# First layer's experts of a two-layer backbone: the row of g2 for each slot comes from a two-row table in DRAM, by a gather per block

## The chip, the cores and the metric

The kernel runs on one core of a Trainium2 chip. The metric is the device time of one execution in microseconds (us); the median of a few runs stands for a kernel.

## The reference, cut to what matters

The backbone has two layers. Each layer mixes tokens and then sends every token through two of 16 experts (a hierarchical mixture of experts). A vector g2 of 1024 numbers scales what the experts add. In the first layer there are two such vectors: one for the 256 context tokens and one for the 1024 latent tokens. In the second layer only latent tokens are left, and so one vector.

```
def expert_block(args):
    xblk, e = args
    return (jax.nn.silu(xblk @ w1[e]) * (xblk @ w3[e])) @ w2[e]
...
out = jnp.zeros((n_tok + 1, d), h.dtype).at[slot_tok].add(yb * slot_w[:, None])
...
if last:
    x = x + g2 * hier_moe(h2, *moe_args).reshape(bsz, n_lat, d)
else:
    f = hier_moe(jnp.concatenate([h2c, h2], axis=0), *moe_args)
    ctx = ctx + cg2 * f[:bsz * n_ctx].reshape(bsz, n_ctx, d)
    x = x + g2 * f[bsz * n_ctx:].reshape(bsz, n_lat, d)
```

The kernel does it slot by slot: each row of an expert's result `y` is multiplied by its slot's weight and by the g2 row of the slot's token, and is added into `xb`, the tokens in DRAM.

## The kernel before

**The expert stage.** It runs from about 940 to 1530 us for the first layer and from about 2320 to 2880 us for the second. The order of the code is the order of the instructions on each engine (a manual schedule). The experts come in the order `eo`, called e0 to e15 here. Every expert has a main block of 128 slots (`block` with `x0`). Ahead of it an expert with many tokens has a full block for its next 128 slots (`x1`) and one more block (`x2`), which is half (64 rows, `block_half`) where few slots are left; an expert with a few tokens too many has one half block; and the others have the main block alone. I call an expert with the main block alone a light one: e0, e2, e4, e6, e8, e12, e14 and e15. In all the first layer runs 29 blocks: 22 of 128 rows and 7 of 64.

**What a main block does.** TensorE forms `hps` from the slots' activations `x` and the weights `ew`, then `yps` (y, in PSUM) from `ghl` and more of `ew`. Each product is made of three matmuls, for which both factors are split into a high and a low part. Around it, `side(u)` prepares the next expert. SyncE fetches its 12 weight units (`eraw`, 512 KB each, 8 buffers). ScalarE copies the high part (L1579). VectorE subtracts for the low part (L1581), for every third unit GpSimd. The rows of later experts are gathered from DRAM on GpSimd's queue (`xg`, L1591 and L1869), and are transposed on TensorE (`xtp`) and split into `x` (L63, L64 and L1611).

**How a block ends.** `gain` makes the row of factors `yt`, and `scatter` multiplies it with y and adds the product into `xb` by an indirect DMA on GpSimd's queue (L1627). The tile `yt` has three buffers, which are given out in the order of the code; as that falls, all main blocks have the same one of the three, and the `x1`, `x2` and half blocks use the others. In the first layer `gain` combines both vectors, which stand broadcast in SBUF: `sw` holds the weight of the slots of latent tokens (0 for the others), `swc` that of context tokens:

```
nc.scalar.activation(out=yt[0:n], in_=g2b[1][0:n], func=AF.Copy, scale=wc[0:n])
nc.vector.scalar_tensor_tensor(out=yt[0:n], in0=g2b[0][0:n], scalar=w[0:n], in1=yt[0:n], op0=OP.mult, op1=OP.add)
...
nc.vector.tensor_tensor(out=yt[0:n], in0=y[0:n], in1=yt[0:n], op=OP.mult)
```

In the second layer there is one vector, and a single operation multiplies y, weight and vector (L1624).

**After the last block** of the first layer comes the second layer's front: SyncE and ScalarE load the tokens back from `xb` (`xf`, L283), ScalarE squares them (L290), SyncE loads weights of the modulation (L241) for TensorE (`modps`, L244), and TensorE transposes the tokens (`tp`, L305).

Of the kernel before, what the change touches and what calls it, by code (L numbers as in the profile page):

```python
# [9 lines left out]
F32 = mybir.dt.float32  # L10
# [10 lines left out]
P = 128  # L21
# [34 lines left out]
def backbone_kernel(ctx: ExitStack, tc: tile.TileContext, x, ctx_in, cond, w_mod, b_mod, norm1, norm2, w_in_t, w_in_vg,  # L56
# [91 lines left out]
    for l in range(depth):  # L148
# [1404 lines left out]
        with ExitStack() as st:  # L1553
# [8 lines left out]
            for c in ((0,) if last else (0, 1)):  # L1562
                g2b[c] = mp1.tile([P, D], F32, name=f"g2{c}")
            swc = sw if last else mp1.tile([P, NB * NE], F32, name="swc")
# [50 lines left out]
            def gain(n, w, wc):  # L1615
                yt = wk.tile([P, D], F32, name="yt", tag="yt", bufs=YT)
                if not last:
                    nc.scalar.activation(out=yt[0:n], in_=g2b[1][0:n], func=AF.Copy, scale=wc[0:n])
                    nc.vector.scalar_tensor_tensor(out=yt[0:n], in0=g2b[0][0:n], scalar=w[0:n], in1=yt[0:n], op0=OP.mult, op1=OP.add)
                return yt  # L1620

            def scatter(yt, y, n, w, yidx):
                if last:
                    nc.vector.scalar_tensor_tensor(out=yt[0:n], in0=y[0:n], scalar=w[0:n], in1=g2b[0][0:n], op0=OP.mult, op1=OP.mult)  # L1624
                else:
                    nc.vector.tensor_tensor(out=yt[0:n], in0=y[0:n], in1=yt[0:n], op=OP.mult)  # L1626
                nc.gpsimd.indirect_dma_start(out=xb, out_offset=bass.IndirectOffsetOnAxis(ap=yidx[0:n], axis=0),  # L1627
                                             in_=yt[0:n], in_offset=None, compute_op=OP.add)

            def block(xt, units, wl_, wc_, yidx, side, s, end=None):  # L1630
# [12 lines left out]
                gs = []  # L1643
                for hf in range(2):
# [16 lines left out]
                for f in range(4):  # L1661
                    w = units[8 + f]
                    for n in range(2):
# [5 lines left out]
                        if (f, n) == (2, 0):  # L1669
                            yt = gain(P, wl_, wc_)  # L1670
# [7 lines left out]
            def block_half(xt, units, wl_, wc_, yidx):  # L1678
# [3 lines left out]
                s = wk.tile([P, D], F32, name="s", tag="yt", bufs=YT)  # L1682
                gs = []
# [37 lines left out]
                yt = gain(R, wl_, wc_)  # L1721
# [98 lines left out]
            for ei, e in enumerate(eo):  # L1820
                x0, x1, x2 = xt_[ei % 2], xt_[2], xt_[(ei + 1) % 2]
                with tc.If(cnt > P + P // 2) as big:
# [8 lines left out]
                    block(x1, units, sw[:, col(e, 1)], swc[:, col(e, 1)], yx[:, col(e, 1)], side1, "e")  # L1831
                    with tc.If(cnt > 2 * P + P // 2) as big2:
                        block(x2, units, sw[:, col(e, 2)], swc[:, col(e, 2)], yx[:, col(e, 2)], idle, "e")
                        with tc.If(cnt > 3 * P):
# [5 lines left out]
                            with tc.For_i(e * cap + 3 * P, e * cap + cnt, P) as i:  # L1840
# [7 lines left out]
                                if not last:  # L1848
                                    nc.vector.tensor_scalar(out=sd[:, 0:1], in0=sd[:, 0:1], scalar1=float(NCTX), scalar2=None, op0=OP.is_lt)
                                    nc.vector.tensor_tensor(out=sd[:, 1:2], in0=sd[:, 0:1], in1=sd[:, 2:3], op=OP.mult)  # L1850
                                    nc.vector.tensor_tensor(out=sd[:, 2:3], in0=sd[:, 2:3], in1=sd[:, 1:2], op=OP.subtract)
                                block(x1, units, sd[:, 2:3], sd[:, 1:2], si[:, 1:2], idle, "e")
                    with big2.Else():
                        with tc.If(cnt > 2 * P):
                            block_half(x2, units, sw[:, col(e, 2)], swc[:, col(e, 2)], yx[:, col(e, 2)])
                with big.Else():
                    with tc.If(cnt > P):  # L1857
                        block_half(x1, units, sw[:, col(e, 1)], swc[:, col(e, 1)], yx[:, col(e, 1)])
# [25 lines left out]
                block(x0, units, sw[:, col(e, 0)], swc[:, col(e, 0)], yx[:, col(e, 0)], side, "")  # L1884
# [139 lines left out]
```

## Time and profile before

| | before |
|---|---|
| median of 3 runs (lowest, highest) | 2894.35 us (2894.32, 2902.83) |
| the profiled execution, its span | 2908.22 us, 2906.5 us |
| busy: TensorE, VectorE, ScalarE, GpSimd | 87%, 63%, 43%, 31% of the span |
| mean granted TensorE clock | 0.934 |

The profile is one execution. Its span is what the rows below are times in, counted from the span's start; 1.7 us of its time lie outside the span. In the rows, an engine's line with a bracket at its end shows how long the engine sat idle before the instruction, and behind `<-` what ended that.

### The profile page before, as it was taken

The page shows a single profiled execution, that of the slowest core. Times are in us where ns is not written, and L with a number is a line of the kernel's source. Part 1 is how long each engine was busy: PE and PEld are TensorE (multiplying, and loading weights), DVE is VectorE, ACT ScalarE, POOL GpSimd, SP SyncE. Part 2 cuts the span into 40 slices and gives each one's busy share as a digit, 9 for nine tenths or more (in the row PEclk, how much of TensorE's full clock was granted, in tenths as well). Part 3 has the DMA queues.
Part 4 walks back from the last instruction along what each step waited for, and adds up shares of the span by engine and source line. Part 5 has one row for each costly group of instructions (what it writes and reads, how often), then busy time and mean ns, then how long its engine had stood idle before and what let it go on. Part 6 is the DMA issues. An engine that isn't in the chain of part 4 may idle for free. (4 is left out here: it accounts for less than half of the span.)

```text
span 2906.5 us, 41486 instructions
## 1 busy us (share of the span) xinstructions
PE 2539.1 (87%) x15412; PEld 2132.5 (73%) x15412; DVE 1816.5 (63%) x3175; ACT 1241.8 (43%) x2060; POOL 898.9 (31%) x576
## 2 busy tenths in 40 slices
PE   6999998898896899889887999979989788878875
PEld 3878887787785677667766898868978666656664
DVE  3304765777478667766775227748857866656765
ACT  3322213566234555544554232137743354545443
POOL 0000113302245444544540001122014445545452
PEclk8999999999897999989998999989989899989987
DMA  8373128331225666776774342173122568686765
GB/s 291 126 246 123 70 86 200 64 71 44 103 109 213 226 223 220 256 252 202 244 243 161 125 141 88 70 181 84 37 89 102 224 222 285 202 279 232 249 234 182
DMA packets 159573, 494.06 MB, mean 170 GB/s; under 512 B 18896, under 2 KB 40016, under 8 KB 158768
## 3 DMA queue, kind: packets, MB, share of 16 engines
q1 hardware_dynamic: 110336, 361.14, 37.5%
q0 software_dynamic: 29312, 99.39, 11.8%
q10 hardware_dynamic: 19552, 28.84, 2.7%
q8 instruction: 200, 3.28, 0.5%
q14 instruction: 173, 1.42, 0.2%
HBM read 408.75 MB, written 79.15 MB: 168 GB/s over the span
## 5 line engine op out<-in xcount | busy, mean ns | idle before, releaser
L1581 DVE TENSOR_TENSOR ew<-eraw,ew 128x1024 fp32r<-128x1024 f32 x256 | 433.7, 1713 | 65.2 <-ACT ew L1579 60.1
L1579 ACT ACTIVATE ew<-eraw 128x1024 fp32r<-128x1024 f32 x384 | 390.5, 1054 | 132.4 <-PE hps L69 115.0
L67 PE MATMUL hps<-ew,x 128*128 128x512 f32 x656 | 281.9, 430 | 105.2 <-PEq L1857 100.6
L1581 POOL TENSOR_TENSOR ew<-eraw,ew 128x1024 fp32r<-128x1024 f32 x128 | 334.4, 2622 | 61.1 <-ACT ew L1579 36.1
L212 PE MATMUL ps<-hh,w 128*128 128x256 f32 x2096 | 289.3, 292 | 17.9 <-ACT hh L319 4.7
L212 PEld LDWEIGHTS ps<-hh,w 128*128 128x128 f32 x2096 | 269.0, 197 | 27.7 <-issue 7.9
L69 PE MATMUL hps<-ew,x 128*128 128x512 f32 x656 | 271.2, 413 | 8.3 <-DVE x L64 7.6
L68 PE MATMUL hps<-ew,x 128*128 128x512 f32 x656 | 271.8, 414 | 0.0
L962 DVE TENSOR_REDUCE mx<-S 128x1 f32<-128x1280 f32 (+1 forms) x144 | 196.8, 1370 | 108.2 <-PE S L957 106.8
L1627 POOL DMA_INDIRECT xb<-yt,yx x54 | 131.2, 2430 | 368.6 <-DVE yt L1626 206.0
L67 PEld LDWEIGHTS hps<-ew,x 128*128 128x128 f32 x656 | 132.6, 202 | 139.7 <-issue 105.7
L970 ACT ACTIVATE pe<-S,mx 128x1280 f32<-128x1280 f32 (+1 forms) x144 | 177.4, 1232 | 49.2 <-DVE mx L962 41.2
L956 PE MATMUL S<-kk,qh 128*128 128x512 f32 (+1 forms) x400 | 159.0, 398 | 16.7 <-DMA qh<-qs 8.3
L69 PEld LDWEIGHTS hps<-ew,x 128*128 128x128 f32 x656 | 132.2, 202 | 41.7 <-DVE x L64 10.2
L68 PEld LDWEIGHTS hps<-ew,x 128*128 128x128 f32 x656 | 133.2, 203 | 28.2 <-issue 1.1
L212 PE MATMUL ps<-hl,w 128*128 128x256 f32 x1048 | 149.1, 286 | 0.0
L67 PE MATMUL ps<-wv,hh 128*128 128x256 f32 (+1 forms) x480 | 142.3, 296 | 0.0
L957 PE MATMUL S<-kk,ql 128*128 128x512 f32 (+1 forms) x400 | 141.4, 368 | 0.3 <-DMA ql<-qs 0.3
L69 PE MATMUL yps<-ew,ghl 128*128 128x512 f32 x328 | 132.5, 404 | 8.0 <-DVE ghl L64 8.0
L67 PE MATMUL yps<-ew,ghl 128*128 128x512 f32 x328 | 138.4, 422 | 0.0
L69 PE MATMUL ps<-wv,hl 128*128 128x256 f32 (+1 forms) x480 | 138.1, 288 | 0.0
L68 PE MATMUL ps<-wv,hh 128*128 128x256 f32 (+1 forms) x480 | 137.9, 287 | 0.0
(597 smaller groups left out, 5765.1 us busy)
## 6 DMA issues: line engine op xcount, KB each, us to landing
eraw<-in_experts_dram SPq DMA_DIRECT2D x384, 512.0 KB
s<-in_w_mod_dram SPq DMA_DIRECT2D x91, 512.0 KB
raw<-in_w_in_t_dram SPq DMA_DIRECT2D x28, 512.0 KB
xb<-xt POOLq DMA_DIRECT2D x18, 512.0 KB, 2.9
h2s<-tm POOLq DMA_DIRECT2D x18, 512.0 KB, 2.9
kk<-ks SPq DMA_DIRECT2D x14, 640.0 KB
ks<-shl ACTq DMA_DIRECT2D x16, 512.0 KB
qs<-shl ACTq DMA_DIRECT2D x16, 512.0 KB
```

Of the source, the lines that this page charges most:

```text
L67: nc.tensor.matmul(o, lhsT=lh, rhs=rh, start=start, stop=False)
L68: nc.tensor.matmul(o, lhsT=lh, rhs=rl, start=False, stop=False)
L69: nc.tensor.matmul(o, lhsT=ll, rhs=rh, start=False, stop=stop)
L212: nc.tensor.matmul(ps[:, o:o + 256], lhsT=wt[:, w_, k, :], rhs=h_[ci][:, k, :], start=w_ == 0 and h_ is hh and k == 0, stop=h_ is hl and k ...
L956: nc.tensor.matmul(S[:, j, :n], lhsT=qh[:, m, q1], rhs=kk[:, m, k0:k0 + n], start=True, stop=False)
L957: nc.tensor.matmul(S[:, j, :n], lhsT=ql[:, m, q1], rhs=kk[:, m, k0:k0 + n], start=False, stop=True)
L962: nc.vector.tensor_reduce(out=u["mx", m], in_=u["S", m], axis=AX.X, op=OP.max, negate=True)
L970: nc.scalar.activation(out=pe[:, :nk], in_=u["S", m], func=AF.Exp, bias=u["mx", m], scale=1.0, accum_out=acc)
L1579: nc.scalar.activation(out=w[:, 0, :], in_=raw, func=AF.Copy)
L1581: eng.tensor_tensor(out=w[:, 1, :], in0=raw, in1=w[:, 0, :].bitcast(F32), op=OP.subtract)
L1627: nc.gpsimd.indirect_dma_start(out=xb, out_offset=bass.IndirectOffsetOnAxis(ap=yidx[0:n], axis=0), in_=yt[0:n], in_offset=None, compute_op ...
```

## The change

It touches the first layer's expert stage alone (`not last`). The two broadcast tiles `g2b` and their two loads of 512 KB are gone, and `swc` with two of its three small operations. A table `rows2` in DRAM holds the two vectors (one DMA of 8 KB), and `kx` holds for each slot the number of its row in it, 1 for a context token. `gain` no longer computes: it gathers for each slot its row of the table into `yt`, by an indirect DMA on GpSimd's queue, and it is called at the start of a block where it was called in the block's last third. `scatter` then multiplies y, the weight and that row in one VectorE operation, as the second layer does with its single vector.

```
+                kx = mp1.tile([P, NB * NE], I32, name="kx")
+                rows2 = dram.tile([2, D], F32, name=f"rows2{l}")
+                nc.scalar.dma_start(out=rows2, in_=modd[l, :, 5 * D:6 * D])
...
-            def gain(n, w, wc):
+            def gain(n, wc):
                 yt = wk.tile([P, D], F32, name="yt", tag="yt", bufs=YT)
                 if not last:
-                    nc.scalar.activation(out=yt[0:n], in_=g2b[1][0:n], func=AF.Copy, scale=wc[0:n])
-                    nc.vector.scalar_tensor_tensor(out=yt[0:n], in0=g2b[0][0:n], scalar=w[0:n], in1=yt[0:n], op0=OP.mult, op1=OP.add)
+                    nc.gpsimd.indirect_dma_start(out=yt[0:n], out_offset=None, in_=rows2,
+                                                 in_offset=bass.IndirectOffsetOnAxis(ap=wc[0:n], axis=0))
                 return yt
...
             def scatter(yt, y, n, w, yidx):
-                if last:
-                    nc.vector.scalar_tensor_tensor(out=yt[0:n], in0=y[0:n], scalar=w[0:n], in1=g2b[0][0:n], op0=OP.mult, op1=OP.mult)
-                else:
-                    nc.vector.tensor_tensor(out=yt[0:n], in0=y[0:n], in1=yt[0:n], op=OP.mult)
+                nc.vector.scalar_tensor_tensor(out=yt[0:n], in0=y[0:n], scalar=w[0:n], in1=(g2b[0] if last else yt)[0:n],
+                                               op0=OP.mult, op1=OP.mult)
...
                 gs = []
+                yt = gain(P, wc_)
                 for hf in range(2):
...
-                        if (f, n) == (2, 0):
-                            yt = gain(P, wl_, wc_)
...
                 s = wk.tile([P, D], F32, name="s", tag="yt", bufs=YT)
+                yt = gain(R, wc_)
                 gs = []
...
-                yt = gain(R, wl_, wc_)
...
             if not last:
-                nc.vector.tensor_scalar(out=swc, in0=ix, scalar1=NCTX, scalar2=None, op0=OP.is_lt)
-                nc.vector.tensor_tensor(out=swc, in0=swc, in1=sw, op=OP.mult)
-                nc.vector.tensor_tensor(out=sw, in0=sw, in1=swc, op=OP.subtract)
+                nc.vector.tensor_scalar(out=kx, in0=ix, scalar1=NCTX, scalar2=None, op0=OP.is_lt)
```

Where it moves instructions is seen on two engines. TensorE's order is the same in both kernels.

On GpSimd a main block of the kernel before looks like this, from the read of the expert's count to the split after the scatter (`xg_11524` is the gather for `x2`; the last DMA is the scatter):

```order
L1872 TENSOR_LOAD cnt_i
L1869 DMA xg_11524<-h2s,ix 128x1024
L1581 TENSOR_TENSOR ew<-eraw,ew 128x1024 x2
L1591 DMA xg<-h2s,ix 128x1024
L1581 TENSOR_TENSOR ew<-eraw,ew 128x1024
L1591 DMA xg<-h2s,ix 128x1024
L1627 DMA xb<-yt,yx 1408x1024
L1581 TENSOR_TENSOR ew<-eraw,ew 128x1024
```

The same place in the changed kernel, whose lines are numbered a few lower or higher (`rows_11526` is the table):

```order
L1621 DMA yt<-rows_11526,kx 128x1024
L1869 TENSOR_LOAD cnt_i
L1866 DMA xg_11524<-h2s,ix 128x1024
L1584 TENSOR_TENSOR ew<-eraw,ew 128x1024 x2
L1594 DMA xg<-h2s,ix 128x1024
L1584 TENSOR_TENSOR ew<-eraw,ew 128x1024
L1594 DMA xg<-h2s,ix 128x1024
L1628 DMA xb<-yt,yx 1408x1024
L1584 TENSOR_TENSOR ew<-eraw,ew 128x1024
```

The new gather stands first, ahead of the gather for `x2` and of all four splits of the block.

On VectorE, the end of e0's main block before, from the split behind `ghl` to the final multiply:

```order
L64 TENSOR_TENSOR ghl<-gtp,ghl 128x256
L1581 TENSOR_TENSOR ew<-eraw,ew 128x1024
L64 TENSOR_TENSOR x_11590<-xtp,x_11589 128x512
L1611 TENSOR_TENSOR x_11589<-xtp,x_11589 128x4x64
L1619 SCALAR_TENSOR_TENSOR yt<-g_11525,sw,yt 128x1024
L1581 TENSOR_TENSOR ew<-eraw,ew 128x1024
L64 TENSOR_TENSOR x_11590<-xtp,x_11589 128x512
L1611 TENSOR_TENSOR x_11589<-xtp,x_11589 128x4x64
L1626 TENSOR_TENSOR yt<-yps,yt 128x1024
```

and in the changed kernel:

```order
L64 TENSOR_TENSOR ghl<-gtp,ghl 128x256
L1584 TENSOR_TENSOR ew<-eraw,ew 128x1024
L64 TENSOR_TENSOR x_11590<-xtp,x_11589 128x512
L1614 TENSOR_TENSOR x_11589<-xtp,x_11589 128x4x64
L1584 TENSOR_TENSOR ew<-eraw,ew 128x1024
L64 TENSOR_TENSOR x_11590<-xtp,x_11589 128x512
L1614 TENSOR_TENSOR x_11589<-xtp,x_11589 128x4x64
L1626 SCALAR_TENSOR_TENSOR yt<-yps,sw,yt 128x1024
```

The operation of L1619 has left the queue, and the split of `ew` moves up into its place. The final operation now reads a tile that a DMA fills.

## Rows read from the trace of the kernel before

**Rows 1.** The page: busy time and share of the span, each engine.

```profile
PE 2539.1 (87%) x15412; PEld 2132.5 (73%) x15412; DVE 1816.5 (63%) x3175; ACT 1241.8 (43%) x2060; POOL 898.9 (31%) x576
```

**Rows 2.** Stretches: length, busy PE PEld DVE ACT POOL, clock, DMA share, GB/s.

```profile
960.00:1526.00 566.00, 501.42 (x2336) 395.74 (x2334) 389.29 (x470) 290.92 (x429) 281.67 (x130) 0.94 0.72 232
...
965.70:971.00 5.30, 5.29 (x13) 4.19 (x14) 2.89 (x4) 2.23 (x3) 4.84 (x4) 0.52 0.99 394
```

**Rows 3.** What TensorE waited for, 955 to 1530 us: total, times, longest.

```profile
PE hps L67 <- PEq L1857: 40.3, 7, 10.4
...
PE hps L69 <- DVE x L64: 6.0, 2, 4.5
PE modps L244 <- DVE yt L1626: 4.3, 1, 4.3
PE yps L69 <- DVE ghl L64: 4.1, 4, 2.2
```

**Rows 4.** Instructions of the lines touched, and the second layer's operation: ns min/median/max.

```profile
L1618 ACT ACTIVATE yt<-g,swc x29: 1137/1147/1166, 957.4 to 1523.5; 128x1024 f32<-128x1024 f32 x22, 64x1024 f32<-64x1024 f32 x7
L1619 DVE SCALAR_TENSOR_TENSOR yt<-g,sw,yt x29: 1266/1285/5399, 958.5 to 1524.7; 128x1024 f32<-128x1024 f32 x22, 64x1024 f32<-64x1024 f32 x7
L1626 DVE TENSOR_TENSOR yt<-yps,yt x22: 1208/1211/1225, 965.9 to 1526.1; 128x1024 f32<-128x1024 f32 x22
L1624 DVE SCALAR_TENSOR_TENSOR yt<-yps,sw,g x18: 1270/1272/1283, 2336.1 to 2855.1; 128x1024 f32<-128x1024 f32 x18
```

**Rows 5.** Gathers: ns; landing us, first of L1869, then of `xg` in 950:1530.

```profile
L1591 POOL DMA_INDIRECT xg<-h2s,ix x64: 942/1757/1950, 919.3 to 2821.9; - x64
...
L1869 POOL DMA_INDIRECT xg<-h2s,ix x30: 937/1058/2007, 957.1 to 2837.5; - x30
...
DMA to landing us min/median/max: 3.8/5.1/6.7
...
DMA to landing us min/median/max: 3.8/8.5/10.4
```

**Rows 6.** Timelines of e0's main block: GpSimd, VectorE, TensorE.

```profile
958.11 4.72 POOL L1581 TENSOR_TENSOR ew<-eraw,ew 128x1024 fp32r<-128x1024 f32 x2
...
958.52 5.40 DVE L1619 SCALAR_TENSOR_TENSOR yt<-g,sw,yt 128x1024 f32<-128x1024 f32 x1
963.85 1.21 DVE L1581 TENSOR_TENSOR ew<-eraw,ew 128x1024 fp32r<-128x1024 f32 x1
964.98 0.68 DVE L64 TENSOR_TENSOR x<-xtp,x 128x512 fp32r<-128x512 f32 x1
...
965.71 0.79 PE L69 MATMUL hps<-ew,x 128*128 128x512 f32 x1 [4.47 <-DVE x L64]
```

**Rows 7.** Timelines of e4's main block, a light one: GpSimd, VectorE, TensorE.

```profile
1109.07 0.97 POOL L1869 DMA_INDIRECT xg<-h2s,ix  x1 [8.13 <-DMA eraw<-in_experts_dram]
1110.06 4.75 POOL L1581 TENSOR_TENSOR ew<-eraw,ew 128x1024 fp32r<-128x1024 f32 x2
...
1125.84 2.34 POOL L1627 DMA_INDIRECT xb<-yt,yx  x1 [4.77 <-DVE yt L1626]
...
1111.15 4.76 DVE L1581 TENSOR_TENSOR ew<-eraw,ew 128x1024 fp32r<-128x1024 f32 x1 [0.53 <-ACT ew L1579]
...
1116.30 0.50 PE L69 MATMUL yps<-ew,ghl 128*128 128x512 f32 x1 [2.19 <-DVE ghl L64]
```

**Rows 8.** Timelines of the layer's end: GpSimd, ScalarE, VectorE, TensorE.

```profile
1510.18 2.33 POOL L1627 DMA_INDIRECT xb<-yt,yx  x1 [6.69 <-DVE yt L1626]
...
1527.56 2.31 POOL L1627 DMA_INDIRECT xb<-yt,yx  x1 [12.63 <-DVE yt L1626]
...
1523.48 1.15 ACT L1618 ACTIVATE yt<-g,swc 128x1024 f32<-128x1024 f32 x1 [4.12 <-DMA xb<-yt,yx]
...
1538.27 1.06 ACT L290 ACTIVATE sq<-xf 128x1024 bf16<-128x1024 f32 x1 [11.75 <-DMA xf<-xb]
...
1526.05 1.23 DVE L1626 TENSOR_TENSOR yt<-yps,yt 128x1024 f32<-128x1024 f32 x1
...
1545.36 1.92 PE L244 MATMUL modps<-xf,condT 128*32 128x512 f32 x4 [11.96 <-DMA xf<-in_w_mod_dram]
```

More of the change, by code (lines that the diff above doesn't have):

```diff
@@ L1561, in backbone_kernel @@
             g2b = {}
[L1562 to L1564 removed]
+            if last:
+                g2b[0] = mp1.tile([P, D], F32, name="g20")
+            else:
+                kx = mp1.tile([P, NB * NE], I32, name="kx")
+                rows2 = dram.tile([2, D], F32, name=f"rows2{l}")
+                nc.scalar.dma_start(out=rows2, in_=modd[l, :, 5 * D:6 * D])
             eo = [EPG * g + i for i in range(EPG) for g in (0, 2, 1, 3)]
@@ L1830, in side1 @@
                             p2(u - 10, ("xtp", "hpse")[u - 10])
-                    block(x1, units, sw[:, col(e, 1)], swc[:, col(e, 1)], yx[:, col(e, 1)], side1, "e")
+                    block(x1, units, sw[:, col(e, 1)], None if last else kx[:, col(e, 1)], yx[:, col(e, 1)], side1, "e")
                     with tc.If(cnt > 2 * P + P // 2) as big2:
-                        block(x2, units, sw[:, col(e, 2)], swc[:, col(e, 2)], yx[:, col(e, 2)], idle, "e")
+                        block(x2, units, sw[:, col(e, 2)], None if last else kx[:, col(e, 2)], yx[:, col(e, 2)], idle, "e")
                         with tc.If(cnt > 3 * P):
@@ L1848, in backbone_kernel @@
                                 if not last:
[L1849 to L1852, printed above, removed]
+                                    kd = wk.tile([P, 1], I32, name="kd", tag="kd", bufs=1)
+                                    nc.vector.tensor_scalar(out=kd, in0=sd[:, 0:1], scalar1=float(NCTX), scalar2=None, op0=OP.is_lt)
+                                block(x1, units, sd[:, 2:3], None if last else kd, si[:, 1:2], idle, "e")
                     with big2.Else():
                         with tc.If(cnt > 2 * P):
-                            block_half(x2, units, sw[:, col(e, 2)], swc[:, col(e, 2)], yx[:, col(e, 2)])
+                            block_half(x2, units, sw[:, col(e, 2)], None if last else kx[:, col(e, 2)], yx[:, col(e, 2)])
                 with big.Else():
                     with tc.If(cnt > P):
-                        block_half(x1, units, sw[:, col(e, 1)], swc[:, col(e, 1)], yx[:, col(e, 1)])
+                        block_half(x1, units, sw[:, col(e, 1)], None if last else kx[:, col(e, 1)], yx[:, col(e, 1)])
                 nxt = []
@@ L1883, in backbone_kernel @@
                     break
-                block(x0, units, sw[:, col(e, 0)], swc[:, col(e, 0)], yx[:, col(e, 0)], side, "")
+                block(x0, units, sw[:, col(e, 0)], None if last else kx[:, col(e, 0)], yx[:, col(e, 0)], side, "")
                 if ei + 1 < NE:
```

## The prediction

> **What bounds the kernel now.** I read the engines' shares first. TensorE is busy for 87% of the span, and no other engine for more than 63% [rows 1]. Then the stage that is changed: of the 566 us from 960 to 1526, TensorE is busy for 501.4, VectorE for 389.3, ScalarE for 290.9, GpSimd for 281.7, and the DMA engines for 0.72 of the time [rows 2]. So TensorE sets the time here too, and an operation taken from another engine gives back at most what TensorE waits for that engine. The waits say how much that is. The largest, 40.3 us in 7 times, is for TensorE's own sequencer after branches, which the change leaves alone. For VectorE's splits of `x` and `ghl` it waited 6.0 + 4.1 = 10.1 us in six times, and 4.3 us at the layer's end for the final multiply [rows 3]. These 14.4 us are all that the removed work can hide in, besides the slower matmuls after a stall: in the 5.3 us after the largest one the granted clock was 0.52, where 0.94 is the stage's mean [rows 2]. At about half the rate 13 matmuls cost some 2.5 us more.
>
> **What goes away.** 29 times ScalarE's 1.15 us (L1618) and 29 times VectorE's 1.28 us (L1619, one of them 5.40) [rows 4]: 33 and about 41 us of busy time, in engines that have 275 and 177 us to spare in the stage. I count them at nothing, except where TensorE stood behind them. That is one place. In e0's block GpSimd runs two splits from 958.11, 4.72 us for both. L1619 starts at 958.52 between them and takes 5.40 us in place of 1.28; behind it stand a split and the `x` for which TensorE sits idle 4.47 us [rows 6].
>
> How much of that comes back? With L1619 gone the next in VectorE's queue is the split L1581, whose input ScalarE delivers at about the same time, and it too would start inside GpSimd's two splits. In e4's block such a split does just that: it starts at 1111.15, inside GpSimd's pair from 1110.06, and takes 4.76 us instead of 1.21 [rows 7, 6]. So I let the split of e0 end where L1619 ended, at 963.9, and `x` comes at 963.9 instead of 964.98. **Term 1: −1.1 us.** Its bounds: nothing, and the whole stall with its slow matmuls, −4.5 − 2.5 = −7.
>
> The Trainium skill, SBUF — State Buffer, section "Who interferes with whom", says that a VectorE instruction with two SBUF inputs and a GpSimd instruction that reads SBUF exclude each other for a whole instruction, whichever comes first. The trace agrees (5.40 us beside 4.72). By that rule the split, which reads `eraw` and `ew` from SBUF, inherits the block, as I count it; were L1619 alone to suffer, the term would be −4.5.
>
> **What is added on GpSimd.** 29 gathers. The nearest rows are the gathers of `xg`: 0.94 to 2.01 us of GpSimd each, 1.06 or 1.76 in the median [rows 5]. So 27 to 58 us are added to an engine with 281.7 of 566 busy. The place counts more than the sum: each gather stands at the head of its block, and in a main block it pushes the gather for `x2` and the splits back by 1 to 1.8 us. The units split late there belong to the next expert, so TensorE doesn't wait for them soon. But the time at which GpSimd's pair of splits falls decides which of VectorE's operations is stretched. In e4 the pair from 1110.06 held VectorE's split until 1115.91, `ghl` came behind it, and TensorE waited 2.19 us [rows 7]. With the pair 1 us later VectorE's split of 1111.15 may come first and run in 1.2 us (the stall goes), or last and end later still (it grows by 1 to 1.8). Four light blocks have this stall, 4.1 us in all; seven of the eight (not e15, which prepares no expert) could have it. **Term 2: 0 us**, between −4.1 and 7 × 1.8 = +12.6.
>
> In a light main block the new gather also has to wait for the previous main block's scatter, which read the same `yt` buffer. That costs nothing new: GpSimd already waits there. In e4 it sat idle 8.13 us until 1109.07, while the block's scatter, which follows the final multiply, began at 1125.84 [rows 7]. That leaves 16.8 us for a gather that lands 3.8 to 10.4 us after its issue [rows 5].
>
> **What is added to the DMA engines.** 22 × 512 KB + 7 × 256 KB = 13.4 MB, against 1 MB of loads less. At 232 GB/s with a share of 0.72 [rows 2] the engines could do about 320; 12.4 MB are 39 us of theirs, a share of 0.07 more in 566 us. Weights are fetched 8 units ahead, so I count it at nothing; that it isn't hidden is part of the rival below.
>
> **The end of the layer.** Here the wait is new, and it lies on the path: the front of the second layer needs the last scatter (ScalarE's `sq` waits 11.75 us for `xf`, TensorE 11.96 us for weights queued behind it) [rows 8]. Before, L1618 of e15 waited for e14's scatter until 1523.48; then came L1619 and the final multiply, which ended at 1527.28 (1526.05 + 1.23), and the scatter at 1527.56 [rows 8]. After, the gather has to wait for the same scatter, until about 1523.4, and then must land. A gather alone in the queue, as L1869's, takes 5.1 us in the median, from 3.8 to 6.7; the wider set of `xg` goes to 10.4 [rows 5]. I take 5.1: this gather has the queue to itself. The row is there at 1528.5, and the multiply of 1.27 us, the second layer's duration [rows 4], ends at 1529.8. **Term 3: +2.5 us**, from 1523.4 + 3.8 + 1.3 = 1528.5 (+1.2) to 1535.1 (+7.8).
>
> The Trainium skill, DMA: Bandwidth & Descriptors, section "Anatomy of one DMA — SWDGE (gpsimd) path", gives a DMA issued from GpSimd about 2.0 us plus its bytes at 436 GB/s. That estimate is 3.2 us for 512 KB and would make the term +0.6; no gather in this trace landed in under 3.8 us, so the rows decide.
>
> **The rest.** The final operation takes 1.27 instead of 1.21 us [rows 4], on the path only at the end and counted there. The table's DMA of 8 KB and the one small operation left of three cost nothing that I can price: TensorE doesn't wait for them.
>
> **The sum.** 2908.22 − 1.1 + 0 + 2.5 = 2909.6 us for an execution like the profiled one, +1.4. That execution lay 13.9 us above the median of 2894.35, so I carry the difference over: 2895.8, say 2896 us. Within 0.3%, 8.7 us, I call two kernels the same.
>
> **The rivals.**
> - **VectorE's relief reaches TensorE: faster.** All six stalls go, 10.1 us, and the slow matmuls after the longer ones, 2.5 + 2 us; the end takes +2.5 back: −12, 2882 us. For it speaks that each of these stalls stands behind a stretched VectorE operation. Against it, that GpSimd's splits, which do the stretching, are all still there.
> - **GpSimd's queue becomes late: slower.** The gathers at the head push the pairs of splits into the places where VectorE makes `ghl`, +1.8 us in each of seven light blocks, and the last gather takes 10.4 us to land: 12.6 + 7.8 = +20, 2915 us. It decides as soon as the pairs cost over 0.9 us a block beside +2.5 at the end (8.7 − 2.5 = 6.2 us in seven blocks). For it: GpSimd already holds VectorE up there. Against: in four of seven blocks only, and for 2.2 us at most [rows 3].
> - **Nothing is seen:** the relief and the new wait both stay under 1 us; 2894. That lies in the same bound as my forecast.
>
> **How the numbers follow.** My forecast, all that ends within 8.7 us, has 0.50 with the third rival in it. The faster rival has 0.20, the slower one 0.30: its bounds are wider and each added gather stands ahead of work. The forecast's own range is 2888 to 2903. For 8 times in 10 the range goes some way into both rivals: 2884 to 2912. Faster by over 0.3%: 0.20; within: 0.50; slower: 0.30.
>
> **What the profile after would show.** Term 1: in e0's block VectorE's split at about 958.5 takes 4 to 5 us, and TensorE's wait for `x` stands at some 3.4 us. Term 2: TensorE's waits for `ghl` in the light blocks still sum to about 4 us, and GpSimd's pairs start 1 to 1.8 us later. Term 3: the last final multiply of the layer waits for a DMA, and it starts about 5 us behind the arrival of e14's scatter. The second layer's experts take as long as before. I am wrong if TensorE waits for `yt` or `yps` in blocks other than the last, if weights come late (waits for `eraw`), or if its waits for its own sequencer change.

## The result, and the profile after

| | before | after |
|---|---|---|
| median (lowest, highest; 5 runs each) | 2900.19 us (2894.32, 2902.83) | 2915.32 us (2911.71, 2916.14) |
| ratio to before, 95% interval | | 1.0059 [1.0043, 1.0076] |
| the profiled execution, its span | 2908.22, 2906.5 us | 2911.71, 2909.9 us |

The change makes the kernel slower by 0.59%, about 17 us (the medians differ by 15). I had predicted 2896, no change. The two profiled executions lie only 3.5 us apart: that of before took longer than any of its five runs in the table, that of after is the fastest of its five. So differences between the two traces tell where time went, and understate how much.

The page's shares, against [rows 1]:

```profile
PE 2541.9 (87%) x15412; PEld 2129.3 (73%) x15412; DVE 1792.1 (62%) x3144; ACT 1214.0 (42%) x2031; POOL 922.0 (32%) x605
```

The stage, with the columns of [rows 2]:

```profile
960.00:1526.00 566.00, 500.79 (x2305) 391.53 (x2304) 358.19 (x437) 261.99 (x398) 295.66 (x154) 0.94 0.75 247
```

VectorE lost 31 us of work and ScalarE 29, GpSimd gained 14, the DMA engines' share rose from 0.72 to 0.75. All of that is as foreseen, and none of it is the time. What TensorE waited for from 935 to 1550 us, against [rows 3]:

```profile
PE hps L67 <- PEq L1854: 37.5, 6, 10.5
...
PE yps L69 <- DVE ghl L64: 10.0, 4, 5.4
PE hps L1687 <- DVE yt L1626: 6.9, 2, 3.5
PE modps L244 <- DVE yt L1626: 5.6, 1, 5.6
PE hps L69 <- DVE x L64: 5.2, 3, 2.1
...
PE hps L1687 <- DVE x L1614: 3.0, 1, 3.0
```

The wait for `ghl` is up from 4.1 to 10.0 us, and one of 3.0 us for an `x` at L1614 (a block of the second expert) is new. The 6.9 us at L1687 are not: before, two waits of half blocks took 6.4 us there (L1686), for `ew`. Most of the first is one place, the main block of expert e14. GpSimd, VectorE and TensorE there, first before:

```profile
1481.79 2.33 POOL L1627 DMA_INDIRECT xb<-yt,yx  x1 [1.72 <-DVE yt L1626]
...
1494.38 0.97 POOL L1869 DMA_INDIRECT xg<-h2s,ix  x1 [7.85 <-DMA eraw<-in_experts_dram]
1495.37 4.75 POOL L1581 TENSOR_TENSOR ew<-eraw,ew 128x1024 fp32r<-128x1024 f32 x2
...
1497.90 3.32 DVE L1581 TENSOR_TENSOR ew<-eraw,ew 128x1024 fp32r<-128x1024 f32 x1 [0.53 <-ACT ew L1579]
...
1501.61 0.50 PE L69 MATMUL yps<-ew,ghl 128*128 128x512 f32 x1 [0.75 <-DVE ghl L64]
```

And after:

```profile
1484.53 2.35 POOL L1628 DMA_INDIRECT xb<-yt,yx  x1 [0.65 <-DVE yt L1626]
...
1498.40 0.97 POOL L1621 DMA_INDIRECT yt<-rows,kx  x1 [9.10 <-ACT x L63]
1499.68 0.94 POOL L1866 DMA_INDIRECT xg<-h2s,ix  x1 [0.30 <-DMA eraw<-in_experts_dram]
1500.64 7.00 POOL L1584 TENSOR_TENSOR ew<-eraw,ew 128x1024 fp32r<-128x1024 f32 x3
...
1500.70 8.03 DVE L1584 TENSOR_TENSOR ew<-eraw,ew 128x1024 fp32r<-128x1024 f32 x1 [0.53 <-ACT ew L1582]
...
1509.13 0.80 PE L69 MATMUL yps<-ew,ghl 128*128 128x512 f32 x1 [5.45 <-DVE ghl L64]
```

Count from the scatter. VectorE's split starts 16.1 us behind it before and 16.2 after. GpSimd's splits start 13.6 us behind it before, 16.1 after: 1.3 us are the new gather with its gap, and 1.3 a later first instruction (12.6 and 13.9 us behind the scatter). Before, the pair had a lead of 2.5 us, so VectorE was held for 2.1 of its 3.32 us. After, GpSimd starts 0.06 us ahead, and a third split is ready by then and follows without a gap: 7.00 us, and VectorE is held for all of it. Behind VectorE's split stands `ghl`, and TensorE waits 5.45 us. Behind the stall the block's last ten matmuls start within 3.92 us; at the 0.23 us a step that the next block has it would be 2.1. The granted clock is 0.64 in the 5.3 us from the stall's end, at its lower level for most of them; before it was 1.00 there. The Trainium skill, SBUF — State Buffer, section "Who interferes with whom", calls the port pair that VectorE and GpSimd share an exclusive lock, held for a whole instruction. The 8.03 us agree, and show in addition that three queued instructions of GpSimd went through before VectorE got its turn.

e0's main block, against [rows 6], VectorE then TensorE:

```profile
952.31 5.93 DVE L1584 TENSOR_TENSOR ew<-eraw,ew 128x1024 fp32r<-128x1024 f32 x1
...
958.90 0.50 PE L69 MATMUL hps<-ew,x 128*128 128x512 f32 x1 [2.11 <-DVE x L64]
```

VectorE is still at e0's last operations there, while TensorE is in the next block already, the second expert's `x1`, and waits for its `x`; so it was before. The split inherited the block, as term 1 had it; the stall fell from 4.47 to 2.11 us. The end of that `x1` block, on GpSimd, VectorE and TensorE:

```profile
963.71 1.65 POOL L1628 DMA_INDIRECT xb<-yt,yx  x1 [0.31 <-DVE g L1657]
...
967.96 0.99 POOL L1621 DMA_INDIRECT yt<-rows,kx  x1 [0.16 <-issue]
...
978.21 1.28 DVE L1626 SCALAR_TENSOR_TENSOR yt<-yps,sw,yt 128x1024 f32<-128x1024 f32 x1 [2.85 <-issue]
...
980.57 0.77 PE L1687 MATMUL hps<-ew,x 128*128 128x512 f32 x1 [2.96 <-DVE x L1614]
```

Here the gather follows e0's scatter at 4 us, and its row is used 10.2 us after its issue. The profile names nothing that ended VectorE's wait of 2.85 us, but y's last matmul starts at 974.67, so the row is what is left to wait for. Behind that operation stand two more that TensorE needs. The gathers in all, and their landing, which the profile tells for 19 of them:

```profile
L1621 POOL DMA_INDIRECT yt<-rows,kx x29: 921/976/1493, 950.2 to 1527.8; - x29
...
DMA to landing us min/median/max: 4.1/6.0/8.0
```

The layer's end, against [rows 8]:

```profile
1527.75 0.98 POOL L1621 DMA_INDIRECT yt<-rows,kx  x1 [7.93 <-ACT ghl L63]
1536.89 2.33 POOL L1628 DMA_INDIRECT xb<-yt,yx  x1 [8.17 <-DVE yt L1626]
...
1535.33 1.28 DVE L1626 SCALAR_TENSOR_TENSOR yt<-yps,sw,yt 128x1024 f32<-128x1024 f32 x1 [7.53 <-DMA yt<-rows,kx]
...
1536.67 4.09 PE L244 MATMUL modps<-s,condT 128*32 128x512 f32 x18 [5.60 <-DVE yt L1626]
```

The last row came 7.6 us after its issue (1527.75 to 1535.33); TensorE's wait there is 5.6 us, against 4.3 before.

### The profile page after: what moved, and what is told of

Its sections match the earlier page's. It is cut to its first block, busy times and chain, and to the rows that moved or that the text cites. A ratio compares the mean times of both kernels' runs of the same rounds, so it can differ in the third digit from the quotient of the medians.

```text
span 2909.9 us, 41459 instructions
## 1 busy us (share of the span) xinstructions
PE 2541.9 (87%) x15412; PEld 2129.3 (73%) x15412; DVE 1792.1 (62%) x3144; ACT 1214.0 (42%) x2031; POOL 922.0 (32%) x605
## 5 line engine op out<-in xcount | busy, mean ns | idle before, releaser
L1584 DVE TENSOR_TENSOR ew<-eraw,ew 128x1024 fp32r<-128x1024 f32 x256 | 452.9, 1788 | 66.3 <-ACT ew L1582 62.0
L67 PE MATMUL hps<-ew,x 128*128 128x512 f32 x656 | 281.7, 429 | 99.6 <-PEq L1854 94.8
L67 PEld LDWEIGHTS hps<-ew,x 128*128 128x128 f32 x656 | 132.0, 201 | 134.6 <-issue 100.0
L67 PE MATMUL ps<-wv,hh 128*128 128x256 f32 (+1 forms) x480 | 142.1, 296 | 0.0
L67 PE MATMUL yps<-ew,ghl 128*128 128x512 f32 x328 | 138.4, 422 | 0.0
```

The source lines that it names most:

```text
L67: nc.tensor.matmul(o, lhsT=lh, rhs=rh, start=start, stop=False)
L1584: eng.tensor_tensor(out=w[:, 1, :], in0=raw, in1=w[:, 0, :].bitcast(F32), op=OP.subtract)
```

## The experiments

The runs are called e1 to e18. Where an expert of the same name is meant, the text says "expert"; e0 is an expert only. All measures stand in one table. Each ratio is to runs of before that were made beside it and had medians of 2894 to 2898 us, so a row's median is not to be held against the 2900.19 of the first row. "Stage" runs from the first layer's first `hps` matmul to the first `tp` after it in the profiled execution; "idle" is the sum of TensorE's gaps over 0.1 us in it, "work" the rest; "held" is the part of idle that ends with `ghl` or `x` of a 128-row product (VectorE's splits held up by GpSimd). "Pair" is the start of GpSimd's pair behind TensorE's first matmul of the block, a mean over the main blocks of experts e2, e4, e12 and e14. I worked these out from the start and gap of each instruction. They belong to one execution each, which lay 8 to 10 us under its kernel's median in e1, e2 and e13 and 7 to 15 over it in before, e6, e11, e14 and e16: differences of a few us between two rows are not resolved.

```
kernel                ratio to before [95%]     median   stage   idle   work  held  pair
before                -                         2900.19  610.7   78.0  532.6  10.8  13.8
after                 1.0059 [1.0043, 1.0076]   2915.32  622.7   83.4  539.3  15.3  14.6
e1_pad                1.0065 [1.0041, 1.0088]   2912.94  618.4   79.2  539.2  15.6  14.9
e2_remove             0.9971 [0.9953, 0.9989]   2888.83  593.2   65.4  527.7   6.3  13.2
e3_add                1.0177 [1.0151, 1.0202]   2950.78  664.9  119.7  545.2  26.8  16.3
e4_later              1.0115 [1.0093, 1.0137]   2930.33  639.2   97.7  541.4   5.5  16.8
e5_delay              0.9984 [0.9966, 1.0002]   2891.07  597.7   68.4  529.3   5.4  13.3
e6_traffic            1.0038 [1.0021, 1.0056]   2905.77  621.4   83.0  538.3  24.5  15.2
e7_prefetch           1.0041 [1.0026, 1.0057]   2907.11  614.7   82.3  532.5  10.2  15.8
e8_pad32              one run                   2917.15  622.4   84.0  538.4  10.3  14.2
e9_small              1.0039 [1.0021, 1.0058]   2905.49  610.6   79.1  531.5  24.5  14.3
e10_raw10             1.0048 [1.0032, 1.0063]   2908.64  617.0   83.8  533.2  11.4  14.5
e11_plain             0.9978 [0.9962, 0.9995]   2888.97  597.9   70.3  527.6   7.5  13.3
e12_align             1.0062 [1.0040, 1.0085]   2912.11  619.8   79.1  540.7  15.8  14.7
e13_delay2            1.0069 [1.0044, 1.0093]   2913.62  620.1   85.8  534.3  26.6  15.1
e14_xg2late           1.0018 [1.0001, 1.0035]   2898.34  608.4   76.1  532.3   6.9  14.1
e15_before_xg2late    1.0008 [0.9989, 1.0026]   2896.24  610.0   74.4  535.6  26.3   -
e16_prefetch6         0.9997 [0.9980, 1.0013]   2893.18  606.1   74.7  531.4  14.7  15.0
e17_xg2late_pad       1.0004 [0.9989, 1.0018]   2896.65  603.3   74.1  529.2  10.5  14.4
e18_best              0.9951 [0.9935, 0.9967]   2883.04  587.4   64.5  522.9   6.0  14.0
```

**The parts of the change alone: e2, e3.** e2 takes the two operations from before and adds no gather. Its factor is that of latent tokens for every row, so context tokens get no contribution (`sw` is 0 for them); the same holds for e5, e6, e9, e11 and e13, which build on it.

```
-   nc.scalar.activation(out=yt[0:n], in_=g2b[1][0:n], func=AF.Copy, scale=wc[0:n])
-   nc.vector.scalar_tensor_tensor(out=yt[0:n], in0=g2b[0][0:n], scalar=w[0:n], in1=yt[0:n], op0=OP.mult, op1=OP.add)
-   nc.vector.tensor_tensor(out=yt[0:n], in0=y[0:n], in1=yt[0:n], op=OP.mult)
+   nc.vector.scalar_tensor_tensor(out=yt[0:n], in0=y[0:n], scalar=w[0:n], in1=g2b[0][0:n], op0=OP.mult, op1=OP.mult)
```

> The kernel before without the two operations of gain and without any gather: the final operation multiplies y, the weight and the latent tokens' vector in one go, so context tokens get no contribution. It is the removal alone, with x at the same addresses as before. Theory of the queue (the loss comes from the gathers' place in GpSimd's queue): the removal gives back only the first stall and pieces, 2 to 5 us: ratio 0.998 to 0.999. Rival, relief: VectorE's and ScalarE's relief is worth 10 us or more (0.9965 or less), and the gathers cost more than 25 us. Second rival: the removal itself costs, since VectorE's splits move into GpSimd's pairs: ratio over 1.002.

The removal is worth 0.3%, 8 us of the medians. So something worth 0.88%, 25 us, stands against it. e3 keeps before's operations and adds a gather of `h2s` rows into `yt` at each block's head.

> The kernel before, with a gather of 512 or 256 KB into yt on GpSimd's queue at the head of each of the 29 blocks (rows of the tokens, overwritten afterwards by gain, which stays). It is the addition alone, with x at the addresses of before. Theory of the queue: the gathers at the head move GpSimd's splits and make VectorE's wait for them, as in the changed kernel: 6 to 12 us slower, ratio 1.002 to 1.004, with a stall of some 5 us for ghl in e14. The last scatter is later too, since L1618 now waits for the gather. Rival, placement alone: ratio 1.000 to 1.001.

It measures another thing: before's ScalarE operation now waits for the gathered tile (38.6 us in 8 waits of ScalarE for `yt` in the stage), and VectorE waits 49.5 us for ScalarE there. The addition can't be priced this way.

**Where the gather stands: e4, e7.** e4 moves the gather of a main block from the head to behind `side(5)`, so that the pair comes first. e7 leaves it early but issues it one main block ahead, at u 10, into two tiles of its own (`ym`).

```
-               yt = gain(P, wc_)
+               yt = gain(P, wc_) if s else None
...
+                       if not s and (hf, u) == (1, 1):
+                           yt = gain(P, wc_)
```

> The changed kernel with the gather of each main block issued behind GpSimd's pair of splits (after side(5)) and not at the block's head; in the x1, x2 and half blocks it stays at the head. x lies as in the changed kernel. Theory of the queue: the pairs start 1 to 1.3 us earlier again, the 5.5 us stall for ghl in e14 shrinks to 1 us and e2's go: 5 to 9 us faster than the changed kernel, ratio about 1.003. Rival, traffic or landing: the ratio stays at 1.006, or the final multiply of the light blocks now waits for the later gather and it is slower still.

> The changed kernel with each main block's gather issued one main block earlier, behind its last split but one and ahead of its scatter, into one of two tiles of its own that lie where the broadcast tiles stood (x lies at the addresses of before). The gathers of the x1, x2 and half blocks stay at their heads. Theory of the queue and of the landing: the pairs are no longer pushed, the last multiply no longer waits, the matmul pitch is 228 ns: 13 to 20 us faster than the changed kernel, ratio 0.998 to 1.001; what is left is the wait in e1's x1 block. Rival, traffic: the same bytes cost the same, ratio 1.003 or more.

In e4 the time held by GpSimd fell to 5.5 us, but the rows came too late: VectorE waited for them, and TensorE for `g` behind it (22.4 us in ten waits). The scatters came late with them: the pair starts 11.2 us behind the scatter instead of 15.6, but 16.8 behind the block's start, later than in after. So e4 shows that late rows cost, and not what an earlier pair is worth. e7 got back only a fifth of what stands against the removal (1.0059 to 1.0041, of 1.0059 to 0.9971), with intervals that overlap. Its pair had no new gather ahead of it, and yet it started later than in after (15.8 against 14.6): with the prefetch issued 1.2 us ahead of the block's scatter, GpSimd waited longer behind that scatter (14.6 us to its next instruction in light blocks, 13.3 in after).

**Delay, bytes or the DMA: e5, e6, e9, e11, e13.** All are e2 with one thing at each block's head that nobody reads: a write of 128x1024 on GpSimd (e5), the 29 gathers from `h2s` (e6), the same gathers with 64 of 1024 columns (e9), a plain DMA of the same bytes on SyncE's queue (e11), two writes (e13).

```
e5    nc.gpsimd.memset(g2b[1][0:n], 0.0)
e6    nc.gpsimd.indirect_dma_start(out=g2b[1][0:n], out_offset=None, in_=h2s, in_offset=...)
e9    nc.gpsimd.indirect_dma_start(out=g2b[1][0:n, 0:64], out_offset=None, in_=h2s.rearrange("n (a b) -> (n a) b", b=64), in_offset=...)
e11   nc.sync.dma_start(out=g2b[1][0:n], in_=h2s[0:n])
e13   for _ in range(2): nc.gpsimd.memset(g2b[1][0:n], 0.0)
```

> The removal alone (as in the run of that name: context tokens get no contribution), plus a GpSimd write of 128x1024 zeros (64 rows in half blocks) into the unused broadcast tile at the head of each block, where the changed kernel has its gather. GpSimd's queue is shifted by about 1 us a block; no DMA is added and nobody waits for the written tile. Theory of the queue: the pairs of splits move as in the changed kernel, VectorE's splits are held up behind them, and 7 to 13 us of what the removal gave are lost: ratio 0.999 to 1.002 against 0.997 of the removal alone. Rival, landing and traffic: GpSimd's queue doesn't matter and the ratio stays at 0.997.

> The removal alone, plus the 29 gathers at the head of the blocks, into a tile that nobody reads (rows of the tokens; context tokens get no contribution). The queue is shifted and the DMA engines carry the same 13 MB as in the changed kernel, but no engine waits for the rows and no gather waits for a scatter. Theory of the queue: as the run with the write, 0.999 to 1.002. Rival, traffic: at least 5 us slower than the run with the write, with longer waits for eraw. Rival, landing: as the removal alone, 0.997; then the loss is in the waits for the rows.

After these two I took the cost for one of traffic, since the write cost almost nothing and the gathers 0.5% more. That was wrong, as the next two show.

> The run of e6_traffic with each of the 29 gathers cut to the first 64 of 1024 columns (256 bytes a row instead of 4 KB, as many rows and as many DMAs; nobody reads them, and tokens of the context get no contribution). The theory that e6 lost its 15 us to the bytes that compete with the expert weights and with the scatters: ratio back near e5_delay's, 0.997 to 1.000, ACT waiting about 10 us in all for eraw and the stage near 598 us. The rival that it is the gather as such (its descriptors, its place in GpSimd's queue): ratio near e6_traffic's, 1.002 to 1.005, eraw waits near 40 us, stage near 620.

> The kernel of e2_remove with a plain DMA of the same size on SyncE's queue (the first 128 or 64 rows of h2s, contiguous, into the unused tile) at the head of each block where e6 had a gather on GpSimd's; tokens of the context get no contribution. If bytes alone cost the 15 us: ratio near e6_traffic's, 1.002 to 1.005. If it is the row-by-row gather or its place in GpSimd's queue, ahead of the scatters: near e2_remove's, 0.996 to 0.999.

A sixteenth of the bytes costs as much, and all the bytes on another queue cost nothing. (The gathers of e6 and e9 are not a copy of the change's: they all write one tile, and in two main blocks they come 8.8 to 9.1 us behind a scatter where the change's come at 3.6.) Then e5 had not delayed what it was meant to delay. In its light blocks GpSimd's first instruction starts 12.1 us behind the scatter and the pair 14.3; in e2 it is 13.3 and 14.4. The write filled a microsecond ahead of the next gather that was empty anyway.

> The kernel of e2_remove with two writes of 128x1024 on GpSimd at the head of each block instead of e5's one (no DMA, nobody reads them; tokens of the context get no contribution). In light blocks GpSimd's pair of splits began 14.1 us after the scatter in before, 14.3 in e5, whose write fell into a microsecond in which the next gather had not begun anyway, and 15.3 to 15.6 in e9, e6 and after. If the place of that pair is what costs: the pair at about 15.2, PE's waits for ghl and x up by 10 us or more over e2, stage 605 to 612, ratio 1.002 to 1.005. If the gather's DMA is what costs, and not its time in GpSimd's queue: as e5, ratio 0.997 to 1.000, stage near 598.

e13 contains no new DMA and is as slow as the changed kernel. A second microsecond on GpSimd takes the ratio from 0.9984 to 1.0069 and the held time from 5.4 to 26.6 us. The pair's place behind the scatter was not as I wrote, though: 13.2 us, since the scatters themselves came later, with all of GpSimd's queue. Behind TensorE's block start it is 15.1, against 13.3. Expert e14's main block in it:

```profile
1499.03 1.97 POOL L1620 MEMSET g<- 128x1024 f32 x2 [5.62 <-DMA xg<-h2s,ix]
1501.18 0.98 POOL L1872 DMA_INDIRECT xg<-h2s,ix  x1 [0.19 <-DMA eraw<-in_experts_dram]
1502.18 7.03 POOL L1581 TENSOR_TENSOR ew<-eraw,ew 128x1024 fp32r<-128x1024 f32 x3
...
1503.19 7.12 DVE L1581 TENSOR_TENSOR ew<-eraw,ew 128x1024 fp32r<-128x1024 f32 x1 [0.53 <-ACT ew L1579]
...
1510.69 0.79 PE L69 MATMUL yps<-ew,ghl 128*128 128x512 f32 x1 [4.54 <-DVE ghl L64]
```

Again three splits of GpSimd run in one go and VectorE is held for all of them: nearly the stall of after the change (4.54 us, there 5.45), made by two writes. The loss is not spread in the same way, though: held time is 26.6 us in e13 and 15.3 in after.

**Late weights: e10.** The changed kernel with `RAW = 8 if last else 10` in layer 0, ten weight buffers in place of eight.

> The changed kernel with ten buffers of fetched weights instead of eight in layer 0 (the two take the 8 KB a partition that the change freed; the context column of the once-per-expert table lies in si instead of a tile of its own; the x tiles stand where they stood before the change). If the loss sits in late weights: eraw waits fall from 19 us to under 10, the stage by 6 to 12 us, ratio 0.999 to 1.003. If it sits in late scatters and the phase of GpSimd's pairs alone: eraw waits fall but the stage stays at 618 to 623 and the ratio at 1.004 to 1.007.

ScalarE's waits for `eraw`, 19.3 us in after, vanish from the list, and the ratio hardly moves (1.0048, in an interval that overlaps after's). Late weights were a symptom.

**The lever: e14, e15, e16.** One number is changed: the gather of `xg2`, which is needed only in the next expert, is issued behind GpSimd's pair in layer 0; in e14 on the changed kernel, in e15 on before. e16 is e7 with the prefetch at u 6.

```
-                   if early and u == 1:
+                   if early and u == (1 if last else 6):
```

> The changed kernel with one number changed: in layer 0 the gather of xg2, which stands at the head of each main block behind the new gather and ahead of GpSimd's pair of splits, is issued at u 6, behind the pair. As many DMAs and bytes as in after. If the place of the pair is what costs: the pair 14.1 to 14.5 us after the scatter in light blocks, e14's stall of 5.45 us under 2, stage 606 to 612, ratio 0.998 to 1.002. If bytes or descriptors of the gathers cost wherever they stand: stage 617 or more, ratio 1.004 or more.

```profile
1491.93 0.98 POOL L1621 DMA_INDIRECT yt<-rows,kx  x1 [8.63 <-DVE x L64]
1492.93 4.74 POOL L1584 TENSOR_TENSOR ew<-eraw,ew 128x1024 fp32r<-128x1024 f32 x2
...
1494.23 4.53 DVE L1584 TENSOR_TENSOR ew<-eraw,ew 128x1024 fp32r<-128x1024 f32 x1 [0.41 <-ACT ew L1582]
...
1499.15 0.50 PE L69 MATMUL yps<-ew,ghl 128*128 128x512 f32 x1 [1.96 <-DVE ghl L64]
```

The same DMAs, in another order: the stall in expert e14's block, shown here, falls from 5.45 to 1.96 us, the ratio from 1.0059 to 1.0018. So the place of one gather in GpSimd's queue carries 0.41 of the 0.59% against before, and just under half of the 0.88% against the removal. Of the 14.3 us by which the stage is shorter, 7.0 are not idle time but work: 64 matmuls of 512 columns, instead of 88, start 0.38 to 0.47 us behind the one before, where 0.23 is the rule.

> The kernel before with the same one number changed (gather of xg2 at u 6 in layer 0), nothing else. If the place of the pair is what costs, the pair comes about 1 us earlier than in before (13.0 to 13.5 us after the scatter), VectorE's split beside it is held less, PE's waits for ghl and x fall from 10.1 us to 4 or less: stage 600 to 606, ratio 0.996 to 0.999. If it doesn't matter: 0.999 to 1.002.

A miss. In light blocks the held time is nearly gone (0.2 us a wait), but in the main blocks of experts with many tokens GpSimd now has no gather to begin with and starts splitting right behind the scatter, into VectorE's splits:

```profile
1066.91 2.89 POOL L1581 TENSOR_TENSOR ew<-eraw,ew 128x1024 fp32r<-128x1024 f32 x1
1069.96 3.17 POOL L1581 TENSOR_TENSOR ew<-eraw,ew 128x1024 fp32r<-128x1024 f32 x1 [0.16 <-POOL ew L1581]
...
1066.45 7.77 DVE L1581 TENSOR_TENSOR ew<-eraw,ew 128x1024 fp32r<-128x1024 f32 x2
...
1075.53 0.79 PE L69 MATMUL yps<-ew,ghl 128*128 128x512 f32 x1 [3.44 <-DVE ghl L64]
```

Held time is 26.3 us, yet the kernel is no slower: TensorE's gaps at the branches (`hps` L67, its sequencer above all) sum to 24.4 us instead of 44.3. The two nearly cancel (15.5 us more and 19.9 less). Whether the one made the other is not shown: in e13, with as much held time, the gaps at the branches still sum to 40.3 us.

> The kernel of e7_prefetch with the gather for the next main block issued at u 6 instead of u 10, well ahead of the scatter instead of 1.2 us before it. In e7 the pair had no new gather ahead of it and yet began 15.3 to 16.5 us after the scatter, as the scatter landed behind the gather. If so: GpSimd free 12.7 to 13.6 us after the scatter, the pair at 13.8 to 14.6, stage 606 to 611, ratio 0.998 to 1.002. If not: pair still above 15, stage near 615, ratio near 1.004.

Within what I had written, except that the pair moved less (13.9 to 15.5 us behind the scatter) and held time stayed at 14.7. What e16 gains over e7 in the traces is in the half and extra blocks, where TensorE's waits fall from 21.1 to 10.8 us.

**The address: e1, e8, e12.** The first product's 512-column matmuls follow each other at 228.3 ns in before and at 233.3 in after (mean from start to start, steps over 0.3 us left out), the second's at 232.4 and 232.9. The freed 8 KB moved the `x` tiles. e1 pads the changed kernel by 8160 bytes a partition to put them back, e8 by 8128, e12 by 8096 with 64 more in the second layer.

```
+                pad = mp1.tile([P, 2040], F32, name="pad")
```

> The changed kernel with a tile of 8160 bytes per partition allocated where the two broadcast tiles of g2 stood, so that the tiles of x lie at the same SBUF addresses as in the kernel before (198592 and up, where the changed kernel has 190432). Nothing else differs. Theory of placement: in the first layer's experts the matmuls into hps follow each other every 233 ns in the changed kernel and every 228 ns in the kernel before because of where x lies; this accounts for 5.1 us of the loss. Then the pitch here is 228 ns and the ratio falls from 1.0059 to about 1.004. Rival, traffic: the gathers' 13 MB slow the matmuls' reads; then the pitch stays at 233 ns and the ratio at 1.006.

> The changed kernel with a pad of 8128 bytes, so that x lies 32 bytes lower than in the kernel before (198560 and up). If the matmul pitch hangs on the address within a few dozen bytes, it is 233 ns as in the changed kernel (whose x addresses leave the same rest by 64, 32); if on the region of SBUF, it stays at 228 ns.

> The changed kernel with the x tiles of layer 0 at byte 198528 of a partition and those of layer 1 at 194368. So far the first product's 512-column matmuls came every 228 ns with the tiles at 198592 and every 233 ns at 198560, 190432 and (layer 1) 194304. If what counts is the address in steps of 128 bytes (198592 is 64 more than a multiple of 128): layer 0 at 233, layer 1 at 228, and layer 1's stage shorter by about 5 us. If it is steps of 64 bytes: both at 228. If it is the layer or the region: layer 0 at 228, layer 1 at 233.

With the tiles back at byte 198592, as in e1, e2, e5 and all others that keep that address, the pitch is 228.2 to 229.0 ns; at 190432 and 198560 it is 233.2 to 233.3, at 198528 it is 230.4, and in the second layer 233.1 to 233.5 at 194304 and 232.7 at 194368. So it follows the address, and not in steps of 64 or 128 bytes: none of e12's three readings came out. In time it is not resolved: e1 is no faster than after.

**Together: e17, e18.** e17 is e14 with e1's pad. e18 is e14 with two tiles of their own for two rows, each fetched at u 6 of the expert before: that of the second expert's `x1` block, and that of the last main block.

```
+                    if u == 6 and not last and ei == 0:
+                        gain(P, kx[:, col(f, 1)], ym[1])
+                    if u == 6 and not last and ei == NE - 2:
+                        gain(P, kx[:, col(f, 0)], ym[0])
```

> The kernel of e14_xg2late with 8 KB a partition of unused padding, so that the x tiles of layer 0 stand at byte 198592, as in before. If the address of the x tiles sets the pitch of the first product: 228 to 230 ns a matmul instead of 233, the stage 4 to 6 us under e14's 608.4, ratio 0.999 to 1.001. If the pitch in e14 had another cause: 233, ratio 1.002.

> The kernel of e14_xg2late with two tiles of their own for the rows of two blocks, fetched at u 6 of the expert before: the extra block of the second expert, whose row came 5.3 us late in e14, and the main block of the last one, at whose end PE waited 6.9 us (1.4 in e2_remove). The two tiles also put the x tiles at byte 198592. If these waits and the address are what is left of the loss: stage 596 to 601, ratio 0.996 to 0.999, faster than before. If waits come back elsewhere: as e17, ratio 0.999 to 1.001.

e17's stage is 5.1 us shorter than e14's, as the address would have it, but the two profiled executions lie 13.5 us apart, and the two ratios' intervals overlap. e18 beats both kernels: 0.9951 [0.9935, 0.9967], about 14 us under before. TensorE's waits from 935 to 1515 us in it:

```profile
PE hps L67 <- PEq L1856: 33.5, 7, 8.7
PE hps L1689 <- DVE yt L1628: 6.9, 3, 3.2
PE yps L69 <- DVE ghl L64: 5.7, 4, 2.2
...
PE modps L244 <- DVE ym L1628: 1.4, 1, 1.4
...
PE hps L1689 <- DVE x L1615: 0.7, 2, 0.3
```

The wait at the layer's end is 1.4 us, as in e2; those for `ghl` and for `x` of the extra block are 4.3 and 2.3 us under after's. By its ratio e18 gains more than the removal alone (0.9971), but the two intervals overlap.

## Why the prediction was wrong

**The mechanism came out as my slower rival had it** ("GpSimd's queue becomes late", 2915 us, chance 0.30). That its total came out too is luck: it had +12.6 us for the pairs and +7.8 at the end, where the traces show +5.9 and +1.3. The forecast lost by one term above all, and by what I held against that rival. Its base was low as well: 2894.35 was the median of three runs, five give 2900.19.

**Term 2 is the step that failed.** I put the shift of GpSimd's pairs at 0, between −4.1 and +12.6 us, as it might help or hurt. It hurt: the waits for `ghl` rose by 5.9 us in the profiled execution, 4.7 of them in expert e14's block alone, where I had allowed 1.8 a block. The bound was wrong because I thought of a pair. When the pair comes later, the third split is ready behind it, and VectorE is held for three. I had also counted a shift of 1 to 1.8 us; there it was 2.5, as GpSimd's first instruction came later too. And I left out the slow matmuls behind a stall, which term 1's bounds and the faster rival have at 2.5 us: those behind this stall cost some 1.8. I also read the four existing stalls of 2.2 us at most as evidence against, when they said only where the pair stood before. The runs e13, with two writes and no DMA, and e14, with the DMAs in another order, show that the place in GpSimd's queue does it. "The units split late there belong to the next expert" was true of the units and beside the point: it is VectorE's next instruction that matters. In the two traces the three terms as measured sum to −2.4 + 5.9 + 1.3 = +4.8 us, still "no change": what they leave out, below, is as large.

**Term 1** had its mechanism right: the split inherited the block. Its size was −2.4 instead of −1.1 in e0. But I had counted the rest of the removed 74 us of work at nothing, and e2 shows 8 us for all of it: held time 10.8 to 6.3, less idle time at the end and at branches, and fewer matmuls at the lower clock behind stalls (work 532.6 to 527.7; these come from an execution 10 us under e2's median and show more than the 8). What VectorE is freed of also moves when its splits meet GpSimd's.

**The DMA traffic at nothing** was right. e11 moves the same bytes at no cost that the runs resolve, e9 costs as much with a sixteenth of them. The longer waits for `eraw` (7.8 to 19.3 us) that I named as a sign of error are there, and e10 takes them away without a gain clear of the noise.

**The wait for the row.** In light blocks it costs nothing, as I had it. I left out the extra block of the second expert, whose gather follows the scatter of e0 after 4 us: 3.0 us of stall there.

**Term 3** was +2.5, from +1.2 to +7.8; the wait grew by 1.3 us, within the bounds. The gather took 7.6 us, not 5.1, but y came later too: its last matmul starts at 1530.68 instead of 1522.69, expert e14's stall included, while the gather was issued 4.3 us after L1618's start before.

**What I did not look at:** the SBUF that the change frees, and with it the address of `x`. The matched matmuls of the two traces run 5 us longer in the stage by pitch alone.

**What stays open.** The two traces account for 12.1 of some 17 us (idle +5.4, work +6.7); the profiled execution of before was a long one, 8.6 us longer than that of after outside the stage, so the rest can't be placed. Whether the 5 us of the address count in time is not settled: e17 against e14 says yes by 0.14% within overlapping intervals, e1 against after says no. And the pair's mean place does not order the kernels by itself (e8 at 14.2 and e18 at 14.0 are far apart in time, and e4, at 16.8, has next to no held time). I take it that what counts is which instruction of VectorE it meets, block by block; the runs show that for the blocks printed here and no others.

## What to carry to other kernels

Where two engines exclude each other, price an added instruction by what it pushes into the other engine's way, up to the longest run of queued instructions, not by its own microsecond: here the second microsecond at a block's head cost 25 us in 29 blocks and the first nothing that the runs resolve. Test such a cost with a plain write of the same length before blaming a transfer. And move what isn't needed yet behind the work that is: one number in the schedule, and two rows fetched earlier, turned a loss of 0.6% into a gain of 0.5%.

## What the runs showed of the hardware

- The pitch of matmuls with identical shapes depended on where the stationary `x` tiles lie in SBUF: 228 to 229 ns with byte 198592, 230 with 198528, 233 with 198560, 190432, 194304 and 194368. What rule stands behind it was not found.
- A VectorE instruction that reads two SBUF tiles waited behind three queued GpSimd instructions in one go: 8.03 us beside 7.00, and 7.12 beside 7.03 in e13, where it takes 1.21 alone.
- A 0.95 us write on GpSimd ahead of a gather cost nothing that the runs resolve (e5 at 0.9984, e2 without it at 0.9971): the first instruction after the idle time started 12.1 us behind the scatter when it was the write (e5), and 13.3 when it was the gather (e2).
